# Output projections in rounds of 1024 rows, and loads moved to GpSimd, in a hybrid decoder layer

## The chip, the cores and the metric

One core of a Trainium2 chip. The metric is the device time of one execution in microseconds (us); the time before is 1065.66 us, the median of three runs (1064.87 to 1065.73). The engines are TensorE (PE, with its weight loads as PEld), VectorE (DVE), ScalarE (ACT), GpSimd (POOL) and SyncE (SP). A trailing q, as in ACTq, is the engine's sequencer, which also issues DMAs.

## The reference, cut to what matters

One decoder layer in fp32, 512 tokens, width 1024, 256 memory tokens, MLP width 4096.

```python
h = rmsnorm(x, norm_mix_g)
proj = h @ w_in                       # conv, stick-breaking attention, retention, three gates
merged = sum(gates * (branches @ w_branch))
x = x + merged @ w_o
h = rmsnorm(x, norm_xa_g)
mem_n = rmsnorm(mem, norm_mem_g)
q = h @ w_q;  k, v = split(mem_n @ w_kv)
x = x + softmax(q @ k.T * XA_HEAD_DIM ** -0.5) @ v @ w_xo      # 4 heads of 256
h = rmsnorm(x, norm_mlp_g)
x = x + square(relu(h @ w_up)) @ w_down
return rmsnorm(x, final_g)
```

The change is about the three products whose result is added into x, w_o, w_xo and w_down, and about the loads of x, of mem and of the gains.

## The kernel before, in words

**Precision.** Every fp32 operand of a large product is split into a high part of fp32r and a rest (`split`, `parts_of`: ScalarE writes the high part on L111 or L265, VectorE subtracts it on L112 or L266), and a product is three matmuls: high by high, high by low, low by high.

**Seven products.** The three output projections save multiplications in Strassen's way (Winograd's form): x's update is cut into a 2 by 2 arrangement of blocks, and seven block products P1 to P7 take the place of eight. `Pairs.make` (L362) forms the left blocks (A11, A22, A12, S1 to S4) from two neighbouring 128-row pieces and splits them; `Wide.step` (L184) forms the right blocks from raw weight chunks (`minus` on L127, `plus` on L130, 128x1024 on VectorE) and splits them. `items_w` (L384) runs the products on TensorE (L403) and after each adds its PSUM bank into x (L409, VectorE, 128x512). P1 and P5 start two PSUM banks each, which P6, P7, P4 and P3 go on with: P1's banks hold P1, then P1 + P6, then P1 + P6 + P7, then with P4, each sum being added to its own quarter of x; P5's banks hold P5, then P5 + P3. P2 has banks of its own. Banks have two tags, `at` (four) and `mm` (four). P1 and P5 use `at`, P2 uses `mm`; `norm_T` (transposes of a normed tile, L499) takes two `at` banks too.

**Rounds.** `Wide1` handles 512 contraction rows a round (four weight chunks of 512 KB), `Wide2` 1024 (eight chunks). w_o and w_xo have two rounds of `Wide1`, w_down four of `Wide2`. A round has 14 adds into x whatever its depth, and per 512 rows seven weight splits, four block sums (two on L127, two on L130) and 84 matmuls of 128x512.

**Order.** The program is a list of items; the compiler's scheduler sets each engine's order from priorities in program order, simulated times and free buffers, so items can overtake one another. Weight chunks come through six buffers (`RAWS`) on SyncE's queue in the order of use, and their split parts go through ten (`WBUFS`, two for each split). Activations share thirty buffers of 4 KB a partition (`UNITS`): the old hT, its mixes, the pairs, x, gains, memory tiles and normed tiles all come from these, and a load starts when its buffer's last reader is done.

**Around the change.** After the gate products, `reload_x` loads x again (four tiles, ACT's queue, L99); `mem_norm` (L927) loads the memory's gain and, one tile after the other, loads (L932), norms and transposes the memory; then w_o in two rounds, with the next norm put behind its second round's products (`ends`, L964), then the key and value products (`kv_proj`). The square sums of a norm are ScalarE's (L468), the power -0.5 is GpSimd's (L462), the scaling VectorE's (L490). In w_xo the last head's output (`xa_out(3)`, L1132) stands between the two rounds. Gains are loaded by `load_g` (L91), on ACT's queue by default.

Of the kernel before, what the change touches and what calls it, by code (L numbers as in the profile page):

```python
# [38 lines left out]
def trunk_kernel(ctx: ExitStack, tc: tile.TileContext, x, mem, par, rot, dqd, kdec, g_mix, g_xa, g_mem, g_mlp,  # L39
# [56 lines left out]
    def load_x():  # L96
        xs = [unit("x", (P, D), F32) for _ in range(NT)]
        for t in range(NT):
            act.dma_start(out=xs[t], in_=x[t * P:(t + 1) * P, :])  # L99
        return xs  # L100
# [69 lines left out]

    ORDER = ("P1", "P5", "P6", "P3", "P2", "P7", "P4")

    class Wide:
# [10 lines left out]
        def step(self, raw, n, j):  # L184
            b11, b12, b22, b21 = (raw[m * self.nb + j] if m * self.nb + j < len(raw) else None for m in range(4))
            if n == 1:
                minus(b11, b12, b11)
            elif n == 2:
                plus(b11, b22, b11)
                plus(b12, b12, b22)  # L190
            elif n == 6:
                minus(b11, b21, b11)
            return parts_of((b11, b11, b11, b22, b21, b12, b11)[n])

    class Wide1(Wide):
        nb = 1

    class Wide2(Wide):
        nb = 2

# [43 lines left out]
    def run_plan():  # L244
        entries, index = [], {}
        for chunks, _ in plan:
            for kind, t, c, *_ in chunks:
                k = (t.tensor.name, c)
                if k not in index:
                    index[k] = kind(t, c)  # L250
                    entries.append(index[k])
        st = S["stream"] = Stream(entries)
        done = 0
        for chunks, fn in plan:
            es = [index[(t.tensor.name, c)] for _, t, c, *_ in chunks]
            for e, (_, _, _, *n) in zip(es, chunks):
                done = max(done, e.last - len(e.steps) + n[0] if n else e.last)
            if es:
                st.pump(done + AHEAD)
            fn(*[e.parts[n[0] - e.nb:n[0]] if n else e.get() for e, (_, _, _, *n) in zip(es, chunks)])  # L260
        plan.clear()
# [92 lines left out]
    class Pairs:  # L354

        def __init__(self, n):
            self.b = [unit("pr_b", (P, 2, 2, 256)) for _ in range(n // 2)]
            self.w = [{} for _ in range(n)]  # L360

        def make(self, e, s, u):  # L362

            def put(names, src):
                w = unit("pr", (P, 2, 2, 256))
                split(w[:, 0], w[:, 1], src)
                for i, n in enumerate(names):
                    self.w[e][n] = w[:, 0, i, :], w[:, 1, i, :]

            v = scr("pr_v", (P, 2, 256))  # L370
            minus(v, u[:, 0:1, :].broadcast_to([P, 2, 256]), s)
            put(("A11", "A22"), s)
            minus(u[:, 0, :], s[:, 0, :], v[:, 1, :])
            put(("S3", "S1"), v)
            hi, lo = self.w[e]["A12"] = self.b[e // 2][:, e % 2, 0, :], self.b[e // 2][:, e % 2, 1, :]
# [7 lines left out]

    def items_w(kind, src, c, pairs, after=lambda p: None):  # L384


        acc, nb = {}, kind.nb
        for n, p in enumerate(ORDER):
            def fn(ws, p=p):
                ws = [wv(w, 2) for w in ws]  # L390
                blocks = pairs().w
                bank = dict(P2="p2", P5="p3", P3="p3").get(p, "p1")
                if p in ("P1", "P5", "P2"):
                    for i in range(2):
                        acc[bank, i] = (mmps if p == "P2" else atps)(bank)

                def mm(i, j):
                    tok = slice(i * P, (i + 1) * P)
                    for k in range(2):
                        ah, al = [x[:, tok] for x in blocks[2 * j + k][LEFT[p]]]  # L400
                        wh, wl = [w[:, k, :] for w in ws[j]]
                        for m, (x, y) in enumerate(((ah, wh), (ah, wl), (al, wh))):
                            te.matmul(acc[bank, i], x, y, start=p in ("P1", "P5", "P2") and j + k + m == 0,  # L403
                                      stop=j == nb - 1 and k == 1 and m == 2, skip_group_check=True)

                def add(i):
                    t, h = TO[p]
                    dst = S["x"][t + i][:, h * 512:(h + 1) * 512]
                    dve.tensor_tensor(out=dst, in0=acc[bank, i], in1=dst, op=ALU.add)  # L409

                if p in ("P7", "P4"):

                    for i in range(2):
                        for j in range(nb):
                            mm(i, j)
                        add(i)
                else:
                    for j in range(nb):
                        for i in range(2):
                            mm(i, j)  # L420
                            if j == nb - 1:
                                add(i)
            item(fn, (kind, src, c, (n + 1) * nb))
            after(p)

# [410 lines left out]
    def gated(n, d, ps2, gt):  # L836
# [8 lines left out]
        if n == 2 and d % 2 == 1:  # L845
            q = d // 2
            if q % 2 == 0:
                S["mp", q // 2] = Pairs(2)
            m = S.pop(("mg", q)).rearrange("p e (h t) -> p (e h) t", h=2)
            S["mp", q // 2].make(q % 2, m[:, 0:4:3, :], m[:, 1:3, :])  # L850
# [74 lines left out]


    def mem_norm():  # L927
        g_bc = load_g(g_mem)
        S["mT"] = Split("mT", KT, MEM)
        for t in range(2):  # L930
            m_sb = unit("m_sb", (P, D), F32)
            act.dma_start(out=m_sb, in_=mem[t * P:(t + 1) * P, :])  # L932
            norm_begin(t, m_sb)
            norm_end(t, m_sb, g_bc)
            norm_T(t, S["mT"], t)

# [75 lines left out]

    item(mem_norm)
    proj_norm(w_o, lambda i: S["mp", i], g_xa, lambda: None, kv_proj)

# [43 lines left out]
    def xa_out(h):  # L1059
        if h % 2 == 0:  # L1060
            S["xo", h // 2] = Pairs(2)
        ph, pl = S.pop(("pT", h))
# [12 lines left out]
    for i in range(KT + 4):  # L1075
# [19 lines left out]
    def u_ready(q, s, u):  # L1095

        act.activation(out=s, in_=s, func=AF.Square)
        act.activation(out=u, in_=u, func=AF.Square)
        if q % 4 == 0:
            S["u", q // 4] = Pairs(4)  # L1100
        S["u", q // 4].make(q % 4, *[x.rearrange("p (a b) -> p a b", a=2) for x in (s, u)])

# [28 lines left out]

    proj_norm(w_xo, lambda i: S["xo", i], g_mlp, lambda: item(lambda: xa_out(3)), first_up)  # L1132

# [11 lines left out]
    def last(p):  # L1145
        if p == "P3":
            def begin():
                S["g"] = load_g(g_fin)
                for t in (0, 1):
# [9 lines left out]
    def down(r):  # L1159
        items_w(Wide2, w_down, 8 * r, lambda: S["u", r], last if r == NP // 4 - 1 else lambda p: None)  # L1160

# [51 lines left out]

def _pack_d(w, nb):


    b = w.reshape(-1, nb, 2, 2, P, 2, 512)
    blocks = [b[:, :, :, k, :, c] for k, c in ((0, 0), (0, 1), (1, 1), (1, 0))]
    return np.stack(blocks, axis=1).transpose(0, 1, 2, 4, 3, 5).reshape(-1, P, CW)

# [7 lines left out]
def _lay_out(i):  # L1228
# [19 lines left out]
        "w_br": np.concatenate([_pack_b(a["w_branch"][0, n]) for n in range(3)], axis=0),  # L1248
        "w_o": _pack_d(a["w_o"][0], 1),
# [3 lines left out]
        "w_xo": _pack_d(a["w_xo"][0], 1),  # L1253
        "w_up": _pack_t(a["w_up"][0][:, :UP * P]),
        "w_up7": _pack_t(a["w_up"][0][:, UP * P:]),
        "w_down": _pack_d(a["w_down"][0], 2),
    }
# [26 lines left out]
```

## Time and profile before

| | |
|---|---|
| median of three runs | 1065.66 us |
| the profiled execution's own time | 1065.17 us |
| its span in the profile | 1062.8 us |
| mean granted TensorE clock | 0.979 |
| DMA | 106.27 MB, mean 100 GB/s |

The profile comes from one execution. A group's line names the line of code, engine, operation, written and read tiles, shape, count, then total and mean duration, then the idle time in front of it and what ended that. A timeline's line is start, duration, engine, line, operation, tiles, count, and in brackets the idle time before it and its releaser. In the waits the three numbers are the sum in us, the number of waits and the longest. In the chain of waits the first two numbers are start and duration of a piece. Windows give busy time and count of each engine in a stretch, then the granted clock, the DMA share and GB/s. The tenths are forty equal slices of the span, 26.57 us each; 9 means 90% or more.

### The profile page before, as it was taken

The numbers are of one execution on the slowest core, as the hardware profiler recorded it, in microseconds if no ns is written. First come the engines' busy times: TensorE is split into PE (matmuls) and PEld (weight loads), VectorE is DVE, ScalarE is ACT, GpSimd is POOL, SyncE is SP. The second block draws the span as 40 slices with busy tenths as digits, with TensorE's granted clock in tenths as the row PEclk, the third lists the DMA queues.
The fourth block names the chain that finished last, engine by engine and source line by source line (L and its number), as shares of the span: only waits on it lengthen the run. The fifth ranks groups of instructions, "written<-read, shape, count | busy, mean of one in ns | idle before, by whom it ended". The sixth has DMA issues, their size and how long they took to land.

```text
span 1062.8 us, 13386 instructions
## 1 busy us (share of the span) xinstructions
PE 1005.8 (95%) x5060; PEld 851.7 (80%) x5060; DVE 752.3 (71%) x1120; ACT 529.4 (50%) x935; POOL 65.4 (6%) x118
## 2 busy tenths in 40 slices
PE   6999999999999999982798999989999999999997
PEld 4888888888888899981688888768888888888885
DVE  5567778866454977894697457995886686587686
ACT  5465567657322354462265345553653553553553
POOL 1011112311000000000010000000000000000001
PEclk9999999999999999996799999999999999999999
DMA  8222232204122122314153411241315205305212
GB/s 317 100 99 80 80 120 80 99 22 137 63 83 76 60 80 99 120 60 178 60 189 128 139 61 40 80 161 38 99 40 179 99 29 189 99 12 195 72 60 80
DMA packets 29872, 106.27 MB, mean 100 GB/s; under 512 B 3568, under 2 KB 3568, under 8 KB 29808
## 3 DMA queue, kind: packets, MB, share of 16 engines
q1 hardware_dynamic: 27216, 98.05, 26.9%
q10 hardware_dynamic: 2592, 7.37, 1.9%
q8 instruction: 40, 0.66, 0.3%
q14 instruction: 24, 0.20, 0.1%
HBM read 103.31 MB, written 2.10 MB: 99 GB/s over the span
## 4 chain that ended last, share of the span: by engine, by line
PE 87%; DVE 8%; DMA 2%; issue 1%; ACT 1%; POOL 0%; SPq 0%; ACTq 0%; DVEq 0%; POOLq 0%
PE mm L277 19%; PE mm L278 19%; PE mm L276 19%; PE p L403 18%; PE p L334 4%; DVE w_part L112 2%; DVE x L409 2%; DMA m_sb<-in_mem_dram 1%; PE at L499 1%; PE o L660 1%; PE aT L626 1%; DVE xn L490 1%; DMA w_raw<-in_w_in_dram 1%; PE z L602 1%; PE z L603 0%
## 5 line engine op out<-in xcount | busy, mean ns | idle before, releaser
L112 DVE TENSOR_TENSOR w_part<-w_raw,w_part 128x1024 fp32r<-128x1024 f32 (+1 forms) x228 | 274.7, 1207 | 155.3 <-ACT w_part L111 141.0
L111 ACT CAST w_part<-w_raw 128x1024 fp32r<-128x1024 f32 (+1 forms) x228 | 235.8, 1040 | 294.3 <-PE mm L277 156.4
L277 PE MATMUL mm<-hT_l,w_part 128*128 128x512 f32 (+1 forms) x704 | 269.0, 382 | 1.3 <-DVE hT_l L266 1.3
L278 PE MATMUL mm<-hT_h,w_part 128*128 128x512 f32 (+1 forms) x704 | 268.9, 382 | 0.0
L276 PE MATMUL mm<-hT_h,w_part 128*128 128x512 f32 (+1 forms) x704 | 268.1, 383 | 0.3 <-ACT hT_h L265 0.3
L403 PE MATMUL p<-w_part,pr 128*128 128x512 f32 x864 | 205.1, 395 | 4.1 <-DVE x L409 4.0
L403 PEld LDWEIGHTS p<-w_part,pr 128*128 128x128 f32 x864 | 163.8, 191 | 39.9 <-ACT xn L468 3.9
L277 PEld LDWEIGHTS mm<-hT_l,w_part 128*128 128x128 f32 x704 | 133.2, 189 | 25.4 <-DVE hT_l L266 1.5
L278 PEld LDWEIGHTS mm<-hT_h,w_part 128*128 128x128 f32 x704 | 133.2, 189 | 24.7
L276 PEld LDWEIGHTS mm<-hT_h,w_part 128*128 128x128 f32 x704 | 132.5, 189 | 24.3 <-ACT hT_h L265 0.5
L409 DVE TENSOR_TENSOR x<-p,x 128x512 f32<-128x512 f32 x112 | 74.8, 683 | 15.6 <-PE p L403 15.3
L462 POOL TENSOR_TENSOR rstd<-ms,half 128x1 f32<-128x1 f32 x18 | 13.0, 723 | 719.0 <-DVE ms L472 675.1
L499 PE MATMUL at<-ident,xn 128*128 128x128 f32 x112 | 18.8, 317 | 36.4 <-DVE xn L490 32.9
L499 PEld LDWEIGHTS at<-ident,xn 128*128 128x128 f32 x112 | 15.1, 164 | 39.1 <-issue 36.4
L403 PE MATMUL p<-w_part,pr_b 128*128 128x512 f32 x144 | 36.8, 404 | 4.7 <-DVE w_part L112 3.1
L127 DVE TENSOR_TENSOR w_raw<-w_raw 128x1024 f32<-128x1024 f32 (+1 forms) x36 | 37.5, 1042 | 1.0 <-DMA w_raw<-in_w_down_dram 0.5
L614 DVE TENSOR_TENSOR_SCAN sb_suf<-ones,sb_e 128x128 f32<-128x128 f32 (+3 forms) x32 | 29.6, 927 | 11.2 <-POOL sb_e L593 9.6
L130 DVE TENSOR_TENSOR w_raw<-w_raw 128x1024 f32<-128x1024 f32 (+1 forms) x36 | 37.4, 1040 | 0.2
L403 PEld LDWEIGHTS p<-w_part,pr_b 128*128 128x128 f32 x144 | 27.9, 196 | 11.6 <-DVE w_part L112 4.0
L334 PE MATMUL p<-mix_h,w_part 128*128 128x256 f32 x192 | 36.8, 283 | 0.0
L334 PEld LDWEIGHTS p<-mix_h,w_part 128*128 128x128 f32 x192 | 30.9, 192 | 0.2
L334 PE MATMUL p<-hT_h,w_part 128*128 128x256 f32 x144 | 28.7, 284 | 1.9 <-DVE sv_s L348 1.5
(219 smaller groups left out, 1486.8 us busy)
## 6 DMA issues: line engine op xcount, KB each, us to landing
w_raw<-in_w_in_dram SPq DMA_DIRECT2D x52, 512.0 KB, 3.5
w_raw<-in_w_up_dram SPq DMA_DIRECT2D x32, 512.0 KB, 3.7
w_raw<-in_w_down_dram SPq DMA_DIRECT2D x32, 512.0 KB, 3.6
w_raw<-in_w_br_dram SPq DMA_DIRECT2D x12, 512.0 KB, 3.5
w_raw<-in_w_gate_dram SPq DMA_DIRECT2D x12, 512.0 KB, 3.5
w_raw<-in_w_o_dram SPq DMA_DIRECT2D x8, 512.0 KB, 3.9
w_raw<-in_w_xk_dram SPq DMA_DIRECT2D x8, 512.0 KB, 3.7
w_raw<-in_w_xv_dram SPq DMA_DIRECT2D x8, 512.0 KB, 4.2
```

The lines of the kernel that those rows point to most:

```text
L111: act.copy(out=wh, in_=src)
L112: dve.tensor_tensor(out=wl, in0=src, in1=wh.bitcast(F32), op=ALU.subtract)
L127: dve.tensor_tensor(out=out, in0=a, in1=b, op=ALU.subtract)
L130: dve.tensor_tensor(out=out, in0=a, in1=b, op=ALU.add)
L276: te.matmul(ps, lh, rh, start=first, stop=False)
L277: te.matmul(ps, lh, rl, start=False, stop=False)
L278: te.matmul(ps, ll, rh, start=False, stop=last)
L334: te.matmul(ps[:, :256], x[:, k, :], y, start=first and k == 0 and i == 0, stop=k == 3 and i == 2, skip_group_check=True)
L403: te.matmul(acc[bank, i], x, y, start=p in ("P1", "P5", "P2") and j + k + m == 0, stop=j == nb - 1 and k == 1 and m == 2, skip_group_check ...
L409: dve.tensor_tensor(out=dst, in0=acc[bank, i], in1=dst, op=ALU.add)
L499: te.transpose(ps[:, k * P:(k + 1) * P], xn[:, c * P:(c + 1) * P], ident)
L614: dve.tensor_tensor_scan(out=suf[:, :s][:, ::-1], data0=ones[:, :s], data1=e1[:, :s][:, ::-1], initial=0.0, op0=ALU.mult, op1=ALU.add)
```

## The change

Six things change:

- w_o and w_xo are done in one round of 1024 rows, as w_down is: `Wide1` and `Wide2` become one `Wide` with two halves j. The host packs the weight chunks in the new order (`_pack_d`).
- The order of the first two products becomes P1 of the first half, P5 of the first half, P1 and P5 of the second half; the other five take both halves in one item. This holds for w_down too.
- `Pairs` holds two pieces with one buffer for A12, and is made for every two pieces; a round takes two of them.
- x, the memory and all later gains are loaded by GpSimd's queue. Both memory tiles are asked for at once, ahead of w_o (`mem_begin`).
- The memory's norm is an item behind P5 of w_o, the transposes of its two tiles stand behind P6 and P3.
- `xa_out(3)` stands ahead of w_xo.

```diff
     def load_x():
         xs = [unit("x", (P, D), F32) for _ in range(NT)]
         for t in range(NT):
-            act.dma_start(out=xs[t], in_=x[t * P:(t + 1) * P, :])
+            pool.dma_start(out=xs[t], in_=x[t * P:(t + 1) * P, :])
...
-    ORDER = ("P1", "P5", "P6", "P3", "P2", "P7", "P4")
+    ORDER = [(p, j) for pair in (("P1", "P5"), ("P6",), ("P3",), ("P2",), ("P7",), ("P4",)) for j in (0, 1) for p in pair]
...
         def __init__(self, t, c):
-            nb = self.nb
-            self.loads = [(t, c + i) for i in range(4 * nb)]
-            self.need = [n * nb + j + 1 for n in (0, 1, 2, 2, 3, 3, 3) for j in range(nb)]
-            self.steps = [lambda raw, n=n, j=j: self.step(raw, n, j) for n in range(7) for j in range(nb)]
+            self.loads = [(t, c + i) for i in range(8)]
+            at = dict(P1=0, P5=1, P6=4, P3=4, P2=6, P7=6, P4=6)
+            self.need = [at[p] + (2 * j if at[p] < 4 else j) + 1 for p, j in ORDER]
+            self.steps = [lambda raw, p=p, j=j: self.step(raw, p, j) for p, j in ORDER]
...
-                if p in ("P7", "P4"):
-
-                    for i in range(2):
-                        for j in range(nb):
-                            mm(i, j)
+                rows = p in ("P7", "P4")
+                for i, j in [(i, j) for i in range(2) for j in js] if rows else [(i, j) for j in js for i in range(2)]:
+                    mm(i, j)
+                    if j == 1:
                         add(i)
-                else:
-                    for j in range(nb):
-                        for i in range(2):
-                            mm(i, j)
-                            if j == nb - 1:
-                                add(i)
-            item(fn, (kind, src, c, (n + 1) * nb))
-            after(p)
+            item(fn, (Wide, src, c, n, n + len(js)))
+
+        for n, (p, j) in enumerate(ORDER):
+            if p in ("P1", "P5"):
+                part(p, [j], n)
+            elif j == 0:
+                part(p, [0, 1], n)
+            if j == 1:
+                after(p)
...
+    def mem_begin():
+        S["g_mem"] = load_g(g_mem, pool)
+        S["m_sb"] = [unit("m_sb", (P, D), F32) for _ in range(2)]
+        for t in range(2):
+            pool.dma_start(out=S["m_sb"][t], in_=mem[t * P:(t + 1) * P, :])
+
     def mem_norm():
-        g_bc = load_g(g_mem)
         S["mT"] = Split("mT", KT, MEM)
         for t in range(2):
-            m_sb = unit("m_sb", (P, D), F32)
-            act.dma_start(out=m_sb, in_=mem[t * P:(t + 1) * P, :])
-            norm_begin(t, m_sb)
-            norm_end(t, m_sb, g_bc)
-            norm_T(t, S["mT"], t)
+            norm_begin(("m", t), S["m_sb"][t])
+            norm_end(("m", t), S["m_sb"][t], S["g_mem"])
+
+    def mem_beside(p):
+        if p == "P5":
+            item(mem_norm)
+        if p in ("P6", "P3"):
+            t = int(p == "P3")
+            item(lambda: norm_T(("m", t), S["mT"], t))
...
-    def proj_norm(src, pairs, g, between, after):
-        items_w(Wide1, src, 0, lambda: pairs(0))
-        between()
+    def proj_norm(src, name, g, beside, after):
...
-                    S["g"] = load_g(g)
+                    S["g"] = load_g(g, pool)
...
-        items_w(Wide1, src, 4, lambda: pairs(1), ends)
+            beside(p)
+        items_w(src, 0, lambda k: S[name, k // 2].w[k % 2], ends)
...
-    item(mem_norm)
-    proj_norm(w_o, lambda i: S["mp", i], g_xa, lambda: None, kv_proj)
+    item(mem_begin)
+    proj_norm(w_o, "mp", g_xa, mem_beside, kv_proj)
...
     item(lambda: xa_out(2))
+    item(lambda: xa_out(3))
...
-    proj_norm(w_xo, lambda i: S["xo", i], g_mlp, lambda: item(lambda: xa_out(3)), first_up)
+    proj_norm(w_xo, "xo", g_mlp, lambda p: None, first_up)
```

More of the change, by code (lines that the diff above doesn't have):

```diff
@@ L256, in run_plan @@
             for e, (_, _, _, *n) in zip(es, chunks):
-                done = max(done, e.last - len(e.steps) + n[0] if n else e.last)
+                done = max(done, e.last - len(e.steps) + n[1] if n else e.last)
             if es:
                 st.pump(done + AHEAD)
-            fn(*[e.parts[n[0] - e.nb:n[0]] if n else e.get() for e, (_, _, _, *n) in zip(es, chunks)])
+            fn(*[e.parts[n[0]:n[1]] if n else e.get() for e, (_, _, _, *n) in zip(es, chunks)])
         plan.clear()
@@ L354, in trunk_kernel, with __init__ @@
     class Pairs:
-        def __init__(self, n):
-            self.b = [unit("pr_b", (P, 2, 2, 256)) for _ in range(n // 2)]
-            self.w = [{} for _ in range(n)]
+        def __init__(self):
+            self.b = unit("pr_b", (P, 2, 2, 256))
+            self.w = [{}, {}]
         def make(self, e, s, u):
@@ L1159, in down @@
     def down(r):
-        items_w(Wide2, w_down, 8 * r, lambda: S["u", r], last if r == NP // 4 - 1 else lambda p: None)
+        items_w(w_down, 8 * r, lambda k: S["u", 2 * r + k // 2].w[k % 2], last if r == NP // 4 - 1 else lambda p: None)
     for q in range(2, NP):
```

64 lines of the change are left out of this document (30 added, 34 removed).

## The prediction

> **What bounds the kernel now.** I read the page first: which engine is full, and in which slice it is not.
>
> ```profile
> span 1062.8 us, 13386 instructions
> PE 1005.8 (95%) x5060; PEld 851.7 (80%) x5060; DVE 752.3 (71%) x1120; ACT 529.4 (50%) x935; POOL 65.4 (6%) x118
> PE   6999999999999999982798999989999999999997
> PEclk9999999999999999996799999999999999999999
> ```
>
> TensorE is the bound nearly everywhere, so only stretches where it stands still can give time back. The 18th to 20th of the slices (each 26.6 us, so 452 to 531 us) are the hole: busy 8, 2 and 7 tenths, the clock down to 6 and 7 tenths in the last two. The waits by sum, and TensorE's own timeline there, say what it is.
>
> ```profile
> PE at L499 <- DVE xn L490: 32.9, 5, 15.5
> ACT xn L468 <- DMA m_sb<-in_mem_dram: 13.5, 2, 10.4
> ```
>
> ```profile
> 476.97 0.28 PE L334 MATMUL p<-hT_h,w_part 128*128 128x256 f32 x1
> 478.83 0.73 PE L403 MATMUL p<-w_part,pr_b 128*128 128x512 f32 x2 [1.58 <-ACT w_part L111]
> 482.48 4.08 PE L403 MATMUL p<-w_part,pr_b 128*128 128x512 f32 x10 [2.92 <-DVE w_part L112]
> 502.02 1.94 PE L499 MATMUL at<-ident,xn 128*128 128x128 f32 x8 [15.46 <-DVE xn L490]
> 511.40 1.94 PE L499 MATMUL at<-ident,xn 128*128 128x128 f32 x8 [7.44 <-DVE xn L490]
> 512.99 7.38 PE L403 MATMUL p<-w_part,pr 128*128 128x512 f32 x24
> ```
>
> After the last gate product (477.25) TensorE runs 12 products of the first w_o round, of P2 (`pr_b` holds only A12), then stands in front of the memory's 16 transposes until 513.0; 156 of the 168 w_o products come behind them. ScalarE's timeline says why the memory is late.
>
> ```profile
> 486.36 1.04 ACT L111 CAST w_part<-w_raw 128x1024 fp32r<-128x1024 f32 x1 [1.02 <-PE p L403]
> 486.65 0.82 ACTq L99 DMA_DIRECT2D x<-in_x_dram  x2
> 489.00 0.50 ACTq L932 DMA_DIRECT2D m_sb<-in_mem_dram  x1
> 498.32 0.63 ACT L468 ACTIVATE xn<-m_sb 128x512 f32<-128x512 f32 x1 [10.40 <-DMA m_sb<-in_mem_dram]
> 504.00 0.33 ACTq L932 DMA_DIRECT2D m_sb<-in_mem_dram  x1
> ```
>
> The loads stand in ScalarE's queue behind a weight cast that waits for TensorE; the second memory tile is asked for only at 504.0, behind the first one's split. Last, the stages by windows, the products (L403) alone in two of them, and rows of the chain and of the timelines that the sums use.
>
> ```profile
> core 0: us, PE busy (x) PEld busy (x) DVE busy (x) ACT busy (x) POOL busy (x), PEclk, DMA share, GB/s
> 477.25:513.00 35.75, 8.35 (x29) 6.42 (x29) 15.73 (x24) 9.43 (x19) 1.11 (x2) 0.62 0.44 161
> 513.00:553.70 40.70, 40.70 (x188) 34.07 (x187) 37.64 (x50) 18.06 (x28) 0.00 (x0) 0.96 0.33 113
> 668.98:718.86 49.88, 45.66 (x191) 36.01 (x190) 48.03 (x73) 24.75 (x44) 1.07 (x2) 0.97 0.40 134
> 718.86:728.60 9.74, 7.69 (x48) 6.83 (x46) 8.41 (x16) 4.84 (x13) 1.10 (x2) 0.82 0.21 68
> 782.62:815.30 32.68, 32.68 (x146) 27.06 (x145) 26.42 (x32) 16.25 (x21) 0.00 (x0) 1.00 0.42 145
> ```
>
> ```profile
> 477.25:553.70 76.45, 42.55 (x168) 33.49 (x168) 0.80 0.38 136
> 668.98:718.86 49.88, 41.86 (x168) 32.08 (x167) 0.97 0.40 134
> ```
>
> ```profile
> 504.00 3.62 DMA m_sb<-in_mem_dram
> 677.97 1.20 DVE x L409 x2
> 782.62 32.64 PE p L403 x144
> ```
>
> ```profile
> 488.69 58.26 SPq L219 DMA_DIRECT2D w_raw<-in_w_xk_dram  x8
> 718.86 1.03 PE L499 MATMUL at<-ident,xn 128*128 128x128 f32 x8
> ```
>
> A product costs TensorE 32.64 / 144 = 0.2267 us, an add into x costs VectorE 0.60 us back to back. The w_o stage lasts 76.45 us for 168 x 0.2267 = 38.1 us of products. The w_xo stage (from 668.98) lasts 49.88 us for the same 38.1, with VectorE busy 96% of it. A w_down round, which has the change's 1024 rows already, fills TensorE without a pause (32.68 of 32.68) over VectorE's 26.42.
>
> **Part A: the w_o stage.** The change takes both waits for the memory (15.46 and 7.44 us) off the path: the loads leave ScalarE's queue, the norm stands beside P5, the transposes behind P6 and P3. They cannot be put ahead of the products again: they need two `at` banks each, P1 and P5 hold all four, and P5's come free only after P3. What limits the stage next? VectorE's work from 477.25 to 553.70 is 15.73 + 37.64 = 53.4 us, the memory's norm and splits included. One round instead of two saves 14 adds x 0.60 = 8.4; 45.0 are left. TensorE needs 38.1 for products, 2 x 1.03 = 2.1 for the transposes at the full clock, and the keys' products that already stood among them: 40.70 - 156 x 0.2267 - (7.38 - 24 x 0.2267) = 3.4, the last bracket being what the first 24 products lost to the slow clock. Together 43.6. So VectorE becomes the longer by a little, and the stage cannot be under 45.0: a gain of at most 31.4. It will not be packed fully; in 513.0 to 553.7 it was busy 37.64 / 40.70 = 92.5%, which gives 48.6.
>
> New in this stage are two waits of the weight stream. With eight chunks in six buffers the last two chunks load only when P3's have been split, as in w_down now. From the waits, the DMA issues, the groups, and GpSimd's timeline:
>
> ```profile
> ACT w_part L111 <- DMA w_raw<-in_w_down_dram: 15.6, 8, 2.6
> L409 DVE TENSOR_TENSOR x<-p,x 128x512 f32<-128x512 f32 x112 | 74.8, 683 | 15.6 <-PE p L403 15.3
> x<-in_x_dram ACTq DMA_DIRECT2D x4, 512.0 KB, 5.2
> m_sb<-in_mem_dram ACTq DMA_DIRECT2D x2, 512.0 KB, 6.5
> 553.87 0.55 POOL L462 TENSOR_TENSOR rstd<-ms,half 128x1 f32<-128x1 f32 x1 [43.94 <-DVE ss L482]
> 554.77 1.59 POOL L462 TENSOR_TENSOR rstd<-ms,half 128x1 f32<-128x1 f32 x1 [0.35 <-DVE ms L472]
> ```
>
> The waits are two a round, 15.6 / 8 = 2.0 us each, on ScalarE; the casts queued behind feed VectorE's splits, which feed TensorE. In w_down VectorE's slack covers it; here there is none, so I charge 2 of the 4 us. The keys' weights, asked for at 488.7 before, now wait for P7's buffers: 1 us more. Stage 51.6, gain 25.
>
> The moved loads: x's first two tiles must be there when P1 and P5 are through, 477.25 + 48 x 0.2267 = 488.1, because P6 goes on in P1's banks and P1's adds come first. Buffers are free from 477.25, when the old hT was last read; with the 5.2 us of the row x is there at 482.5. Issued as late as before (486.65) it would cost 3.8 us. The memory comes behind four x tiles and the gain vector: before, its first tile was usable 498.32 - 486.65 = 11.7 us after the first issue and its transposes stood 502.02 - 498.32 = 3.7 us later; with the second tile 3.6 to 4 us behind (its 3.62 after issue), 477.25 + 19.4 = 496.7, and P3 ends near 477.25 + 96 x 0.2267 + some 3 = 502. Covered, with 5 us to spare.
>
> No load in this trace is issued by GpSimd, so its price has two ends: ScalarE's 0.82 / 2 = 0.41 us, and that plus what a GpSimd instruction lost beside VectorE, 1.59 - 0.55 = 1.04 us at 554.77. Seven loads at the dear end come 7.3 us later and overrun the spare by 2; if the buffers too come free only at 486.65, 9.4 later, the memory costs 11. I take nothing, since TensorE has 5 us in hand, and keep 11 for the range. [...]
>
> **Part B: the w_xo stage.** VectorE's 48.03 lose 14 adds, 8.4, and become 39.6. TensorE needs 38.1 and 23 other matmuls (191 - 168), 5.2 at most: 43.3. So TensorE is the bound, and at most 49.88 - 43.3 = 6.6 us are to be had.
>
> ```profile
> 668.98 0.40 PE L403 MATMUL p<-w_part,pr_b 128*128 128x512 f32 x1
> 688.55 0.68 DVE L266 TENSOR_TENSOR pr<-xo_s,pr 128x512 fp32r<-128x512 f32 x1
> 714.45 4.57 PE L403 MATMUL p<-w_part,pr 128*128 128x512 f32 x12 [3.52 <-DVE x L409]
> ```
>
> The stall in the last row, behind VectorE's backlog of adds, goes. The clock stands at 0.82 in 718.86 to 728.60 after it; kept full that is up to 9.74 x 0.18 = 1.75 us more, I take 1. What comes instead: the second half of P1 needs the last head's blocks. Without them TensorE has 24 products and the 23 others, 10.7 us, to 679.7. If that block (688.55 + 0.68) were as late as now, it would wait 9.5 us; if the head's matmuls, now ahead of the products in the program, come as early as their inputs, nothing. I take 2.5, nearer to nothing because splits and adds of the old first round filled VectorE there. Gain 6.6 - 2.5 + 1 = 5, ends -2.9 and 8.3.
>
> **The rest.** w_down keeps its 168 products and 14 adds a round; the new order of P1 and P5 is covered by VectorE's 6.3 us of slack per 32.68. Without that cover a late split would cost its 2.0. g loads on GpSimd: nothing, they have a product to land in.
>
> **Sum.** 25 + 5 = 30 us off the profiled execution's own 1065.17 (span 1062.8 and 2.4 around it; 0.5 under the median of the runs): 1035. The ends of the parts, 31.4 + 8.3 and (25 - 11) - 2.9, give 1025.5 and 1054.
>
> **The rivals.**
> 1. The memory's transposes stay a wait, shorter and in a new place: TensorE's queue is in order, and they stand ahead of P2, P7 and P4. For it: the GpSimd issue is unpriced, and buffers could come free later than 477.25. Against: the 5 us in hand. It costs 2 to 11, so 1037 to 1046. Chance 0.15.
> 2. w_xo waits for the last head: 9.5 instead of 2.5 us, 1042. For it: 24 products are little to hide behind, where a whole round stood before. Chance 0.13.
> 3. The change does not move the wait: the order of instructions is the compiler's, and it put P2 ahead of the memory although the program had it behind. If products still queue behind the memory, only the earlier loads and fewer adds are left: 1055 to 1064. Against: the four banks. Chance 0.05.
> 4. Slower: GpSimd's issue is starved by a full VectorE. With d per load, the second memory tile is ready at 477.25 + 7d + 3.6 + 3.7 against 502 for P3 (3.6 being the 3.62 of the chain's row, 3.7 the norm). TensorE's loss passes the 30 us from d = 6.8 us on; at 8 us it is 38.6 and the time 1074. Against: this needs over six holds of 1.04 us per load. Chance 0.07.
>
> **How the numbers follow.** My forecast has 0.60 and lies within 1026 to 1041. Rival 1 reaches 1046, rival 2 1042, both together 1053; I put the range to 1050, which leaves out rivals 3 and 4 and a little of each side. 0.2%, 2.1 us, is about what a measurement of this kernel can tell from no change. Faster: 0.60 + 0.15 + 0.13 + 0.03 of rival 3 = 0.91; slower: 0.06 of rival 4; the same: the remaining 0.03.
>
> **What would show it.** L409 x84 instead of x112. TensorE's busy tenths with no 2 in the 19th slice and a clock of 9 throughout; no wait of over 4 us for `xn` in front of L499. The w_o stage some 50 us from last gate product to last product, VectorE over 90% busy in it; P2's casts waiting about 2 us for `w_raw<-in_w_o_dram`. The w_xo stage near 45 us, without the 3.52 us stall. The memory landing before 497. I am wrong if TensorE stands before L499 or before P6 for over 6 us, or if w_xo is not shorter.

## The result, and the profile after

The changed kernel takes 1033.53 us (median of 4, 1031.67 to 1035.21); the kernel before, on the same chip, 1065.26 (1064.86 to 1065.73). The ratio is 0.9702, with a 95% interval of 0.9683 to 0.972: 32 us less, where 30 were forecast. The profiled execution took 1034.26 us, its span is 1032.5. A second profiled execution of the same kernel, called the repeat below, has a span of 1029.9, and its time over 4 runs was 1033.25 us, ratio 0.971 (0.9695 to 0.9725).

The page of after: the first lines, the products' engine by slices, its clock.

```profile
span 1032.5 us, 13357 instructions
PE 1000.0 (97%) x5060; PEld 846.0 (82%) x5060; DVE 732.8 (71%) x1092; ACT 529.3 (51%) x935; POOL 69.2 (7%) x128
PE   5999999999999999998999998999999999999996
PEclk9999999999999999999899999999999999999999
L405 DVE TENSOR_TENSOR x<-p,x 128x512 f32<-128x512 f32 x84 | 56.8, 684 | 20.5 <-PE p L399 20.4
```

The hole of 8, 2 and 7 tenths is closed, the clock stays up but for one 8, and the adds are 84 instead of 112. In the numbering of after the products are L399, the adds L405, the transposes L496. The longest waits left before TensorE, besides those at the start of the kernel:

```profile
PE xpp L1054 <- DVE x_p L1046: 3.7, 1, 3.7
PE p L399 <- ACT pr L260: 2.7, 1, 2.7
PE p L399 <- ACT w_part L111: 2.4, 1, 2.4
```

The second and third are in the w_o stage, the first in w_xo. TensorE's timeline of the w_o stage:

```profile
469.85 2.65 PE L399 MATMUL p<-w_part,pr 128*128 128x512 f32 x11
...
481.56 2.79 PE L399 MATMUL p<-w_part,pr 128*128 128x512 f32 x11 [0.34 <-ACT gt L885]
487.07 2.90 PE L399 MATMUL p<-w_part,pr 128*128 128x512 f32 x10 [2.72 <-ACT pr L260]
493.31 5.90 PE L399 MATMUL p<-w_part,pr_b 128*128 128x512 f32 x12 [2.40 <-ACT w_part L111]
...
515.10 0.60 PE L496 MATMUL at<-ident,xn 128*128 128x128 f32 x4
```

The memory's transposes (515.10, and three more groups up to 522.65) have no bracket: nothing waits for them. Two short stalls stand at the front instead: P1's second half waits for the last pair's A11, and P2 for its weight cast. The chain of waits of after says where they come from: from 469.40 to 488.60 nearly all its steps are VectorE's, and its end is

```profile
487.45 1.15 DVE w_part L112
488.61 3.50 DMA w_raw<-in_w_o_dram
493.31 1.22 PE p L399 x2
```

By the chain, the end of VectorE's split at 487.45 lets the load of P2's chunk start (chunks come through six buffers); the cast and P2 come behind. From 493.31 on the chain is TensorE's. To see what each stage gave, take two steps of the chain that are the same work in both kernels: a group of softmax transposes (`xpp`) between the two stages, and w_down's first round. First the chain of before (its w_down step, 782.62, is in the prediction), then of after, then of the repeat.

```profile
662.83 0.44 PE xpp L1051 x4
```

```profile
633.75 0.45 PE xpp L1054 x4
752.12 32.64 PE p L399 x144
```

```profile
631.49 0.45 PE xpp L1054 x4
749.48 32.64 PE p L399 x144
```

The first shift is 662.83 - 633.75 = 29.1 us, what the w_o stage and the stretch behind it (the next norm, the keys, the queries) gave together. The second is 782.62 - 752.12 = 30.5, so w_xo gave 1.4. In the repeat the same two shifts are 31.3 and 33.1. Forecast were 25 for the w_o stage alone and 5 for w_xo: the sum held, its parts are taken up below. TensorE's timeline of w_xo, and VectorE's in front of it, say why the second is so small.

```profile
641.39 0.74 PE L273 MATMUL mm<-xpT,xv_l 128*128 128x512 f32 x2 [0.73 <-DVE xv_l L261]
645.87 0.66 PE L1054 MATMUL xpp<-ident,x_p 128*128 128x128 f32 x2 [3.75 <-DVE x_p L1046]
646.18 5.97 PE L399 MATMUL p<-w_part,pr 128*128 128x512 f32 x17
642.98 1.22 DVE L130 TENSOR_TENSOR w_raw<-w_raw 128x1024 f32<-128x1024 f32 x1
645.38 0.61 DVE L1046 TENSOR_SCALAR x_p<-x_p,x_sm 128x256 f32<-128x256 f32 x2
```

The old stall of 3.52 us is gone, and a new one of 3.75 stands at the other end of the stage. The last step of the last head's softmax (L1046) is behind weight work on VectorE; its transposes wait for it, and the products stand behind them in TensorE's queue. The 17 products that follow take 5.97 us, against 17 x 0.2267 = 3.9 at the full clock.

Last, GpSimd's timeline, on which three rivals hung.

```profile
468.29 2.56 POOL L99 DMA_DIRECT2D x<-in_x_dram  x4 [116.68 <-PE mm L273]
475.56 0.54 POOL L928 DMA_DIRECT2D m_sb<-in_mem_dram  x1 [0.37 <-PE p L329]
```

An issue takes 0.54 us (0.64 as the mean of x's four), and x is asked for 18 us earlier than before (468.29 against 486.65).

### The profile page after: what moved, and what is told of

It is laid out like the page before. It is cut to its first block, busy times and chain, and to the rows that moved or that the text cites. A ratio compares the mean times of both kernels' runs of the same rounds, so it can differ in the third digit from the quotient of the medians.

```text
span 1032.5 us, 13357 instructions
## 1 busy us (share of the span) xinstructions
PE 1000.0 (97%) x5060; PEld 846.0 (82%) x5060; DVE 732.8 (71%) x1092; ACT 529.3 (51%) x935; POOL 69.2 (7%) x128
## 4 chain that ended last, share of the span: by engine, by line
PE 92%; DVE 4%; DMA 1%; ACT 1%; issue 1%; SPq 0%; POOL 0%; DVEq 0%; POOLq 0%; ACTq 0%
PE p L399 21%; PE mm L272 20%; PE mm L273 20%; PE mm L271 20%; PE p L329 5%; DVE w_part L112 1%; PE o L657 1%; PE at L496 1%; PE aT L623 1%; DMA w_raw<-in_w_in_dram 1%; PE z L599 1%; PE z L600 0%; DVE w_raw L130 0%; PE ro L804 0%; PE sc L778 0%
## 5 line engine op out<-in xcount | busy, mean ns | idle before, releaser
L399 PE MATMUL p<-w_part,pr 128*128 128x512 f32 x864 | 206.2, 394 | 3.8 <-ACT pr L260 2.7
L399 PEld LDWEIGHTS p<-w_part,pr 128*128 128x128 f32 x864 | 162.7, 190 | 40.3 <-ACT pr L260 3.1
L405 DVE TENSOR_TENSOR x<-p,x 128x512 f32<-128x512 f32 x84 | 56.8, 684 | 20.5 <-PE p L399 20.4
L399 PE MATMUL p<-w_part,pr_b 128*128 128x512 f32 x144 | 37.1, 411 | 2.4 <-ACT w_part L111 2.4
L399 PEld LDWEIGHTS p<-w_part,pr_b 128*128 128x128 f32 x144 | 28.5, 199 | 9.5 <-ACT w_part L111 2.8
L465 ACT ACTIVATE xn<-x 128x512 f32<-128x512 f32 x32 | 20.0, 628 | 19.4 <-DVE x L405 16.2
L614 ACT ACTIVATE sb_suf<-sb_suf 128x128 f32<-128x128 f32 (+3 forms) x32 | 15.1, 471 | 27.7 <-DVE sb_suf L613 27.7
L329 PE MATMUL p<-mix_l,w_part 128*128 128x256 f32 x96 | 27.1, 283 | 0.0
```

Source lines behind the costliest of these rows:

```text
L329: te.matmul(ps[:, :256], x[:, k, :], y, start=first and k == 0 and i == 0, stop=k == 3 and i == 2, skip_group_check=True)
L465: act.activation(out=dst[:, cs], in_=src[:, cs], func=AF.Square, accum_out=ss[:, i:i + 1])
```

## The experiments

The theory: the time came from the memory's wait in w_o, which had two causes (late loads, and the norm's place in front of the products), and w_xo gave little because one stall took the place of another. Its rivals: that the round of 1024 rows is the main part, that GpSimd as the issuing engine is, that VectorE limits the stage.

**The memory alone, the rounds alone.** The first kernel is the one before with the memory's part only (loads, `mem_begin`, `mem_norm` and `mem_beside` as in the change; the edit is cut to the calls).

```diff
-    item(mem_norm)
-    proj_norm(w_o, lambda i: S["mp", i], g_xa, lambda: None, kv_proj)
+    item(mem_begin)
+    proj_norm(w_o, lambda i: S["mp", i], g_xa, lambda: None, mem_beside, kv_proj)
```

> The kernel before with the memory's part alone: residual, gain and memory loads issued by GpSimd, the memory's norm beside P5 and its transposes behind P6 and P3 of the first round; both projections stay in two rounds. Theory (the two waits of 15.46 and 7.44 us go, but VectorE keeps its 14 adds more, 53.4 us of work in the w_o stage, which at 92.5% packing takes 57.8 of the 76.45 us): 18.7 us less, about 1046; the rounds are then worth some 12 us on top. Rival (the memory's wait is all there was to gain and VectorE is no second limit): 24 to 29 us less, 1036 to 1041. Second rival (the waits hid other work and only move): 10 us less or under, 1055 or more.

Measured: 1044.45 us, ratio 0.9818 (0.9802 to 0.9834). The theory's size came; its reason was another, see below. The second kernel is the changed one with the memory as before.

```diff
-    item(mem_begin)
-    proj_norm(w_o, "mp", g_xa, mem_beside, kv_proj)
+    item(mem_norm)
+    proj_norm(w_o, "mp", g_xa, lambda p: None, kv_proj)
```

> The changed kernel with the memory's part as it was before: loads on ScalarE, memory norm and transposes in front of the products. Theory: the TensorE waits for the memory stay, 20 us or more, and behind them TensorE was full already in the kernel before (40.70 of 40.70 us), so the 8.4 us of adds saved in w_o give nothing by themselves; 0 to 4 us less than before, 1061 to 1065. Rival (one round is itself the main part of the 32 us): 1050 or less.

Measured: 1060.66 us, 0.997 (0.9958 to 0.9982). As the theory had it: 3 us less. One part gives 1.8%, the other 0.3%, both together 3.0%: some 9 us come only when both are there. TensorE's timeline of the memory's part alone shows them, with VectorE's beside it:

```profile
482.06 2.57 PE L403 MATMUL p<-w_part,pr_b 128*128 128x512 f32 x10 [0.16 <-DVE w_part L112]
494.33 17.62 PE L403 MATMUL p<-w_part,pr 128*128 128x512 f32 x66 [9.70 <-DVE x L409]
492.98 0.69 DVE L266 TENSOR_TENSOR pr<-mg,pr 128x512 fp32r<-128x512 f32 x1 [0.68 <-ACT pr L265]
493.59 3.33 DVE L409 TENSOR_TENSOR x<-p,x 128x512 f32<-128x512 f32 x5
```

P1, P5 and P2 of the first round have run by 484.6, but P1's adds stand in VectorE's queue behind the last pair's blocks, and P6 needs the banks that those adds free. That is one wait of 9.70 us. The other reading of the 9 us is the work, 14 x 0.60 = 8.4 us, that a second round's adds give VectorE. To tell the two apart, the adds of that round were left out:

```diff
+                    if src is not w_o or c > 0:
-                    dve.tensor_tensor(out=dst, in0=acc[bank, i], in1=dst, op=ALU.add)
+                        dve.tensor_tensor(out=dst, in0=acc[bank, i], in1=dst, op=ALU.add)
```

> The kernel before with the memory's part alone, and the 14 adds of w_o's first round left out, so that the residual lacks that round's products. Theory (what two rounds cost once the memory is out of the way is one wait of 9.70 us: P6 of the first round needs P1's banks, whose adds stand in VectorE's queue behind the last block pair's work): that wait goes, 8 to 11 us less than the memory's part alone, 1033 to 1037. Rival (the second round's stalls take its place, or the adds cost by their number, 14 x 0.60 us): 0 to 5 us less, 1039 to 1045.

Measured: 1033.34 us, 0.9711 (0.9697 to 0.9724), 11 us less than the memory's part alone and level with the changed kernel. The work went together with the wait here, so it is the size that parts them: 11 us is more than 8.4, and about the wait with the slower products behind it (66 in 17.62 us, against 66 x 0.2267 = 15.0). In its timeline nothing interrupts the products where the wait was:

```profile
486.66 16.03 PE L403 MATMUL p<-w_part,pr 128*128 128x512 f32 x70
```

In the changed kernel no product waits for these adds either. There P6 comes behind 48 products of P1 and P5 instead of 24; that this is what covers the adds is read from the program and not tested by itself.

**Is VectorE the limit of the w_o stage?** The forecast had it as the longer engine. Here the changed kernel leaves out all 14 adds of w_o:

```diff
-                    dve.tensor_tensor(out=dst, in0=acc[bank, i], in1=dst, op=ALU.add)
+                    if src is not w_o:
+                        dve.tensor_tensor(out=dst, in0=acc[bank, i], in1=dst, op=ALU.add)
```

> The changed kernel without the 14 adds of w_o into x: the products are computed and left in their banks, so the residual goes on without this projection. VectorE has 14 x 0.60 = 8.4 us less to do in the stage, and no product waits for an add. Theory (in the stage as it came out VectorE is busy 38.28 of 45.01 us and is no limit any more; what is lost is two early stalls and the slow clock behind them): 0 to 3 us less than the changed kernel, 1030 to 1033. Rival (the forecast's step: VectorE is the longer engine of the stage): 6 to 8.4 us less, 1025 to 1027.

Measured: 1032.09 us, 0.9698 (0.9685 to 0.9711), the same as the changed kernel: 8.4 us less work for VectorE gave at most 1 or 2. But the trace is not that of the changed kernel with fewer adds. P6 has no adds to wait for, P2 comes behind P6 and P3, its 2.40 us wait is gone, and the last w_o product ends at 520.3 instead of 526.0. Then a new wait takes most of that back, with slower keys' products behind it (0.41 us each and some 0.21 apart, against 0.28 and 0.12 from 527.46 on):

```profile
486.92 15.27 PE L399 MATMUL p<-w_part,pr 128*128 128x512 f32 x60 [2.69 <-ACT pr L260]
524.22 1.11 PE L496 MATMUL at<-ident,xn 128*128 128x128 f32 x4 [2.26 <-DVE mT_l L261]
```

So VectorE's work as a sum does not set the time. It does not follow that VectorE is never the limit: the stall for A11, at the front, is the same 2.69 us, and the first add of the changed kernel runs only at 494.43, behind it.

**The loads and the place of the norm.** Two kernels of the changed kind, one with the loads on ScalarE, one with the norm in front.

```diff
-            pool.dma_start(out=xs[t], in_=x[t * P:(t + 1) * P, :])
+            act.dma_start(out=xs[t], in_=x[t * P:(t + 1) * P, :])
...
-            pool.dma_start(out=S["m_sb"][t], in_=mem[t * P:(t + 1) * P, :])
+            act.dma_start(out=S["m_sb"][t], in_=mem[t * P:(t + 1) * P, :])
```

> The changed kernel with the seven loads of the w_o stage (and the other gain loads) issued by ScalarE at the same places of the program. Theory (the place in ScalarE's queue counts, behind the cast of the last block pair): the first x load is issued near 487 instead of 468 us and lands near 492, P1's adds and with them P6 wait 2 to 6 us; 1036 to 1040. Rival (an issuing engine is worth its issue time only, 7 x 0.41 = 2.9 us of an engine that is busy half the time): within 1 us of the changed kernel, 1033 to 1034.5. In both the memory is in time for its transposes, since in the changed kernel its squares waited till 505.8 for other reasons.

Measured: 1035.3 us, 0.9731 (0.9716 to 0.9745). That lies between theory and rival, some 2 us above the changed kernel, at the edge of what these intervals part. The wait that the theory foretold is there, with its size. Its timelines of ScalarE's queue and TensorE:

```profile
490.40 1.95 ACTq L99 DMA_DIRECT2D x<-in_x_dram  x4
495.56 5.28 PE L399 MATMUL p<-w_part,pr 128*128 128x512 f32 x12 [4.07 <-DVE x L405]
```

x is asked for 22 us later, P6 waits 4.07 us for P1's adds, and the stage makes half of it good: no product waits for P2's weight cast any more, where the changed kernel waits 2.40 us. Two stalls one behind the other do not add up.

```diff
     item(mem_begin)
+    item(lambda: [mem_norm()] + [norm_T(("m", t), S["mT"], t) for t in (0, 1)])
-    proj_norm(w_o, "mp", g_xa, mem_beside, kv_proj)
+    proj_norm(w_o, "mp", g_xa, lambda p: None, kv_proj)
```

> The changed kernel with its early loads on GpSimd, but the memory's norm and transposes in front of the products in the program, as before the change. Theory (the wait had two causes, the late loads and the place; with the memory landed by 482 us and VectorE full to 494 us, the transposes still stand in TensorE's queue for the norm): 4 to 12 us more than the changed kernel, 1037 to 1045. Rival A (the place alone is what counts): 20 us more or over, 1053 to 1061. Rival B (the early loads alone are what counts): within 1.5 us, 1032 to 1035.

Measured: 1044.4 us, 0.9815 (0.9801 to 0.9828), as the theory had it. Its timelines of GpSimd, ScalarE, VectorE and TensorE:

```profile
472.75 0.54 POOL L928 DMA_DIRECT2D m_sb<-in_mem_dram  x1 [0.37 <-PE p L329]
488.78 0.62 ACT L465 ACTIVATE xn<-m_sb 128x512 f32<-128x512 f32 x1
489.53 0.15 DVE L479 TENSOR_SCALAR ss<-ss 128x1 f32<-128x1 f32 x1
492.49 1.94 PE L496 MATMUL at<-ident,xn 128*128 128x128 f32 x8 [13.75 <-DVE ss L479]
```

The last memory tile is asked for at 472.75, but the norm's first square sum runs on ScalarE at 488.78, behind the last pair's casts, its first step on VectorE at 489.53, and the transposes hold up every product for 13.75 us. The four kernels in one round per projection side by side:

| memory's norm | loads on ScalarE | loads on GpSimd |
|---|---|---|
| in front of the products | 1060.66 | 1044.4 |
| beside the products | 1035.3 | 1033.53 |

The loads alone are worth 16 us, the place alone 25; with the norm beside the products the loads' engine is worth some 2. The first cell differs from its neighbour in more than the engine: there, as before the change, the second memory tile is asked for only behind the first one's norm. What of the 16 us is the engine and what the early asking was not separated.

**w_xo.** Three kernels: w_xo alone in two rounds again, P1 and P5 without turns (in every projection), and the last head moved.

```diff
-        items_w(src, 0, lambda k: S[name, k // 2].w[k % 2], ends)
+        if name == "xo":
+            items_h(src, 0, lambda: S[name, 0])
+            item(lambda: xa_out(3))
+            items_h(src, 4, lambda: S[name, 1], ends)
...
-    item(lambda: xa_out(3))
```

(`items_h` is the loop of before, one round of 512 rows, with w_xo packed as before.)

> The changed kernel with w_xo alone back in two rounds of 512 rows, the last head's output between them. Theory (landmarks of the two profiles: the w_xo stage gave only 1.4 us, since the 3.52 us stall behind VectorE's adds and the slow clock were exchanged for a 3.75 us stall before the last head's transposes): 0 to 2 us more than the changed kernel, 1034 to 1036. Rival (the forecast's 5 us is what the merged w_xo is worth, and the landmarks mislead): 1037 to 1039. Second rival (the round of 84 products was the better cover for the last head): 1 to 3 us less, 1030 to 1032.

Measured: 1032.63 us, 0.9703 (0.969 to 0.9716): the same as the changed kernel. The merged w_xo is worth nothing as it stands. Its timeline has the old stall back, and no stall for the last head:

```profile
685.19 3.00 PE L451 MATMUL p<-w_part,pr 128*128 128x512 f32 x12 [3.55 <-DVE x L455]
```

```diff
-    ORDER = [(p, j) for pair in (("P1", "P5"), ("P6",), ("P3",), ("P2",), ("P7",), ("P4",)) for j in (0, 1) for p in pair]
+    ORDER = [(p, j) for pair in (("P1",), ("P5",), ("P6",), ("P3",), ("P2",), ("P7",), ("P4",)) for j in (0, 1) for p in pair]
...
-            self.need = [at[p] + (2 * j if at[p] < 4 else j) + 1 for p, j in ORDER]
+            self.need = [1, 3, 3, 4] + [at[p] + j + 1 for p, j in ORDER[4:]]
```

> The changed kernel with P1's two halves ahead of P5's two halves in the program, chunks loaded in the same order. Theory (the compiler orders the products by when their inputs are ready, and puts P5's first half ahead of P1's second half by itself): within 1 us of the changed kernel, 1032.5 to 1034.5. Rival (the halves in turn are what covers the last pair's A11, 2.72 us late in w_o, and the last head's, in w_xo): 12 products of 0.2267 us less cover in each stage, 2.7 to 5.4 us more, 1036 to 1039.

Measured: 1032.01 us, 0.9699 (0.9686 to 0.9713): the same. The halves in turn are not needed in the program; in both kernels 36 of w_o's 48 products of P1 and P5 run before the wait for the last pair's blocks (487.07 in after, 487.38 here), so the first products of P5 stand ahead of the end of P1's second half all the same. The last kernel moves two items of the last head:

```diff
-        if 0 <= h < XH:
+        if 0 <= h < XH and (h, tp) != (3, 1):
             item(lambda h=h, tp=tp: xa_transpose(h, tp))
...
-    item(lambda: xa_out(3))
+    n_xo = len(plan)
...
     proj_norm(w_xo, "xo", g_mlp, lambda p: None, first_up)
+    plan.insert(n_xo + 1, ((), lambda: xa_transpose(3, 1))); plan.insert(n_xo + 3, ((), lambda: xa_out(3)))
```

> The changed kernel with the last head's last transposes placed behind P1's first half and the last head's output behind P5's first half of w_xo (the program before the change had that output between the rounds). Theory (the 3.75 us wait for x_p and the slow clock after it, about 2.4 us, come from the transposes standing in TensorE's in-order queue ahead of 24 products that were ready): 3 to 6 us less than the changed kernel, 1028 to 1031. Rival (VectorE is the limit there, full from 639.9 to 645.9, and any order of TensorE meets the same end): within 1 us of the changed kernel, 1033 to 1034.5. Second rival (the last head's blocks then come too late for P1's second half): 1 to 4 us more.

Measured: 1030.1 us, 0.9687 (0.9669 to 0.9704), which overlaps the changed kernel's interval; so both ran once more, side by side.

> The changed kernel once more, beside the kernel with the last head placed later, on one chip. Both theories: 1032 to 1034.

> The kernel with the last head's last transposes and output placed later, once more. Theory (its profile's span was 4.1 us shorter than the changed kernel's, all of it in the w_xo stage): 3 to 4 us less than the changed kernel on the same chip. Rival (the profiled runs differ by chance as the times did, whose intervals overlapped): within 1 us of it.

Measured: 1033.25 us for the changed kernel, 0.971 (0.9695 to 0.9725), and 1029.43 for the moved head, 0.967 (0.9657 to 0.9683). The intervals are apart: 3.8 us less, as the theory had it, and the fastest kernel of this study. From its waits and its chain:

```profile
PE xpp L1054 <- DVE x_p L1046: 0.8, 1, 0.8
```

```profile
632.77 0.44 PE xpp L1054 x4
747.25 32.64 PE p L399 x144
```

The wait for the last head's softmax is 0.8 instead of 3.7 us. The shifts against before are 30.1 and 35.4, so w_xo now gives 5.3 us.

**GpSimd for sums.** One step further, P6's sums of w_o and w_xo went from VectorE to GpSimd, on top of the moved head:

```diff
-                plus(b11, b22, b11)
-                plus(b12, b12, b22)
+                e = dve if self.loads[0][0] is w_down else pool
+                for o, x, y in ((b11, b22, b11), (b12, b12, b22)):
+                    e.tensor_tensor(out=o, in0=x, in1=y, op=ALU.add)
```

> The kernel with the last head's transposes and output placed later, and besides it P6's two sums of each half, in w_o and w_xo alone, computed by GpSimd instead of VectorE. Theory (the early stalls, 2.72 us for the last pair's A11 and 2.40 us for P2's cast, come from VectorE being full with weight work from 474 to 494 us): 4 x 1.22 = 4.9 us of that work goes, the stalls shrink, 1 to 4 us less than the kernel with the head placed later, 1026 to 1029. Rival (GpSimd takes much longer for a 128 x 1024 sum or holds VectorE up, and P6 waits for it, or the x loads stand behind the sums in its queue): 2 us more or worse, 1032 and up.

Measured: 1038.08 us, 0.9754 (0.9741 to 0.9767), some 8 us more than with the sums on VectorE: the rival. Its timelines of GpSimd, VectorE and TensorE:

```profile
474.53 12.02 POOL L192 TENSOR_TENSOR w_raw<-w_raw 128x1024 f32<-128x1024 f32 x3 [3.98 <-DVE w_part L112]
486.49 2.36 POOL L99 DMA_DIRECT2D x<-in_x_dram  x4
478.83 2.18 DVE L112 TENSOR_TENSOR w_part<-w_raw,w_part 128x1024 fp32r<-128x1024 f32 x1 [0.50 <-ACT w_part L111]
481.53 2.82 DVE L112 TENSOR_TENSOR w_part<-w_raw,w_part 128x1024 fp32r<-128x1024 f32 x1
490.00 5.10 PE L400 MATMUL p<-w_part,pr 128*128 128x512 f32 x12 [5.87 <-ACT pr L261]
500.37 5.27 PE L400 MATMUL p<-w_part,pr_b 128*128 128x512 f32 x12 [5.27 <-ACT w_part L111]
```

By the trace a sum takes GpSimd about 12.02 / 3 = 4.0 us here (2.6 in w_xo, as the mean of the four: the eight take 24.9 us, w_o's four 2.47 + 12.02) against VectorE's 1.22, VectorE's splits beside it take 2.18 and 2.82 instead of 1.22, and x is asked for only behind the sums. The two early stalls grow from 2.72 and 2.40 us to 5.87 and 5.27. Which of the three costs most was not separated, and whether less work for VectorE at the front would shorten these stalls is not shown: no run made that work less without another engine taking it over.

## Why the prediction was right, and where its parts were not

**The main point held.** The memory's waits were the price of w_o, and placing the norm beside the products took them away. Of the signs named these came: 84 adds; no 2 among the slices and a clock of 9, but for one 8; no wait for `xn` in front of w_o's transposes; the memory there before 497 (asked for at 475.56, landing 5.7 us after issue by the median of its row, so 481). P2's cast waited 1.10 us for its chunk, where about 2 were named, and the stage from last gate product to last product lasted 45.0 us, where some 50 were named. Two signs failed, VectorE over 90% busy and w_xo near 45 us (49.88 - 1.4 = 48.5), and they belong to the two steps that were off.

**Part A, 25 forecast: the size came, the reason did not.** The step that failed is "So VectorE becomes the longer by a little, and the stage cannot be under 45.0", with the 92.5% packing put on it. The window of after from the end of the gate products to the end of w_o's (busy time of TensorE, of its weight loads, VectorE, ScalarE, GpSimd; then the clock):

```profile
480.83:525.84 45.01, 39.25 (x162) 30.24 (x161) 38.28 (x55) 24.21 (x43) 3.60 (x5) 0.92 0.36 129
```

That it lasts 45.01 us, just the floor, is chance: VectorE is busy 38.28 us of it, 85%, and idle 6.7. Its work was not bound to the stage: 24 of the 168 products ran among the gate products from 466.90 on, which end 3.6 us later for it, and their weight splits ran ahead of them. VectorE was full at the front (10.07 of 10.07 us from 480.83 to 490.90), and by the chain that is where it set the time; behind 493.31 TensorE did. The two waits of the weight stream, charged at 2 us, came as one: P2's cast waited 1.10 us for its chunk, and TensorE 2.40 for the cast. ScalarE's row:

```profile
492.21 1.04 ACT L111 CAST w_part<-w_raw 128x1024 fp32r<-128x1024 f32 x1 [1.10 <-DMA w_raw<-in_w_o_dram]
```

The 2.72 us wait for the last pair's A11 was in no term.

The 29.1 us of the first shift are not all the stage's. From the end of w_o's products to the step of the chain, before and after:

```profile
553.70:662.83 109.13, 106.01 (x604) 93.38 (x603) 67.97 (x122) 52.68 (x109) 4.80 (x4) 0.98 0.29 98
525.84:633.75 107.91, 107.83 (x633) 95.37 (x632) 69.34 (x121) 54.23 (x111) 1.07 (x2) 1.00 0.31 108
PE at L499 <- DVE hT_l L266: 3.1, 2, 2.7
```

This stretch is 1.2 us shorter, and it holds the keys' products, 3.4 us by the prediction's sum, that ran among w_o's before. So some 4.6 us were gained behind the stage: the next norm's transposes waited 3.1 us before (the last row) and wait no more, and the clock stays full. The prediction put nothing there, and no run tells why the wait went; the keys' products that now stand beside these transposes may cover it. That leaves 24.5 us for the stage (26.7 in the repeat). In the prediction's terms, from 477.25 and with the keys' 3.4, the stage lasted 3.6 + 45.0 + 3.4 = 52.0 us, against 51.6: a floor from the sum of VectorE's work, which was none, stood for stalls and slow clock that were not listed. And the whole, 24.5 + 4.6 + 1.4 = 30.5 against 30, came close because a term at nothing made up for most of what w_xo missed. Both are luck.

**Part B, 5 forecast, 1.4 and 1.8 measured.** The step that failed is the choice of 2.5 us for the last head, "nearer to nothing because splits and adds of the old first round filled VectorE there". The mechanism, rival 2's, was named; its size was wrong and it came one place earlier than thought, at the transposes and not at P1's second half. It cost 3.75 us of stall and 2.1 of slow clock (5.97 - 3.9 above; the granted clock was 0.50 from 646 to 649); another wait behind VectorE, 0.73 us, stands just ahead. With the head moved w_xo gives 5.3.

**w_down and the g loads: nothing**, as forecast: w_down's rounds last 32.64 us in both kernels.

**The rivals.** 1 (memory late behind GpSimd's loads) fell: no wait in front of L496 in the stage. 2 came in part, with a size near 6 us, between the 2.5 and the 9.5 of the prediction. 3 (the program's place does not count) fell: front against beside is 11 us with the early loads. 4 (issue starved by VectorE) fell: 0.54 us an issue. VectorE's rows between 473 and 477 us, where the gain vector and the memory were issued in after, are two-input TENSOR_TENSOR, one behind the other (0.41 to 1.22 us each), and the three issues beside them took 0.54 us each. Beside a sum of GpSimd's, in the kernel that has them, VectorE's splits took 2.18 and 2.82 us instead of 1.22. The issuing engine made some 2 us where the norm stands beside the products. With the norm in front moving the loads brought 16 us, far more than the issue time (3.3 us for the seven on ScalarE's queue in the kernel of the rounds alone), since the end of the loads was waited for there (9.51 and 2.83 us); but the early asking for both tiles is in these 16 us too.

## What to carry to other kernels

Before a stall is priced, ask what stands in each engine's queue ahead of the work that ends it: here the loads stood behind a cast, the adds behind block work, the products behind transposes, and in each case another order, or more products ahead of the wait, took it away. Do not set an engine's total work in a window as a floor for the window, unless nothing of that work can run earlier; look instead where in the window the engine is full. Before a shift between two kernels is put down to one stage, see whether the same work lies ahead of the step in both. When a stage is shortened from one end, list what its new first instructions wait for; the gain of w_xo was lost there, and two moved items brought it back.

## What the runs showed of the hardware

Two executions of the same program with nearly the same stalls ran the same 12 products of P2 in different times. Windows of after and then of the repeat, TensorE alone (busy time, clock, DMA):

```profile
487.00:493.00 6.00, 3.58 (x12) 1.00 0.34 102
493.00:499.00 6.00, 5.65 (x12) 0.50 0.46 162
```

```profile
487.00:493.00 6.00, 4.47 (x12) 0.74 0.33 94
493.00:499.00 6.00, 4.93 (x21) 1.00 0.51 171
```

P2's products are the 12 of the second row in the first execution and among the 21 of the second row in the second; the first rows hold the end of P1 and P5. In the first the granted clock was 0.50 over 493 to 499, and P2's products took 5.90 us, some 3 more than 12 x 0.2267 = 2.7. In the second it was 0.74 over 487 to 493, ahead of P2's wait (were the slow part at the 0.50 of the first, some 3 us of it: 6.00 x 0.26 / 0.5, an estimate), P2's products took 0.73 + 2.54 = 3.3 us, and the first shift came out 2.3 us larger (31.34 against 29.08). So part of a stage's time is not the program's. In the first the clock fell with no wait longer than 2.72 us in front of it in the stage, in the second with none longer than 2.69.
